# Moving the on-chip tiles of a one-core transformer-layer kernel to other places modulo 512 bytes, by pads

## The chip, the cores and the metric

The kernel runs on one core of one Trainium2 chip. The metric is the time of one execution on the device in microseconds (us); smaller is better. Each time is a median of several runs. Beside the timed runs there is one profiled execution, whose trace gives each instruction's start and shown length.

The engines are named as in the profile: PE is TensorE (matmuls and transposes), PEld its loading of weights, DVE is VectorE, ACT is ScalarE, POOL is GpSimd, SP is SyncE (which issues DMAs). All but PE's results, which go to PSUM, lies in SBUF: 128 partitions, in each of which a tile has a start address and a number of bytes.

## The reference

One layer of a hybrid decoder on x of shape (1, 1024, 1024), all in float32, with a feed-forward width of 2816:

```python
xn = rmsnorm(x, norm_mix_w[l])
proj = xn @ w_in[l]
da_q, da_k, da_v, sw_q, sw_k, sw_v, g_da, g_sw = split_cols(proj)
...
y_da = diff_attention(da_q, da_k, da_v, lam, lam_init, subln_w[l])
y_sw = sliding_window_attention(sw_q, sw_k, sw_v, sinks[l])
merged = jax.nn.sigmoid(g_da) * (y_da @ w_br_da[l]) + jax.nn.sigmoid(g_sw) * (y_sw @ w_br_sw[l])
x = x + merged @ w_mix_out[l]
xn = rmsnorm(x, norm_ffn_w[l])
x = x + conv_ffn(xn, w_up[l], conv_w[l], conv_b[l], w_down[l])
...
return rmsnorm(x, norm_final_w)
```

The matrix products with `w_in`, the two branch weights, `w_mix_out`, `w_up` and `w_down` hold nearly all of the arithmetic.

## The kernel before, in words

**A product.** Every float32 operand is split into a high and a low part of type fp32r (`xh`, `xl` of an activation, `wh`, `wl` of a weight), and a product is the sum of three matmuls: high by high, high weights by low activations, low weights by high activations. In `mm3` these are lines 150, 151 and 152, in `product` lines 835, 836 and 837. The weights are 128 x 128, the moving operand is 128 partitions by 512 columns of 4 bytes (2048 bytes a partition), and the result is one PSUM bank.

**Strassen-Winograd.** Pairs of output tiles in `project` (nine pairs), in `hidden` (22 rounds) and in the middle of `down` are computed with seven half-size products P1 to P7 in place of eight. The weight operands are `A11`, `A12`, `A22` (slices of the weights as they are) and `S1` to `S4` (sums and differences of them, tiles `sh` and `sl`, made in `split_pair`, L101). The moving operands are `B11`, `B21`, `B22` and `T1` to `T4`. The order in a round is P1, P2, P5, P6, P7, P3, P4, with 12 matmuls each; in the last pair or round another order holds.

```python
prods = (("P1", "A11", "B11"), ("P2", "A12", "B21"), ("P5", "S1", "T1"), ("P7", "S3", "T3"),
         ("P3", "S4", "B22"), ("P6", "S2", "T2"), ("P4", "A22", "T4"))
```

**The stages**, in order of time:

- `project`: x by `w_in`. Three plain tiles first (`blocks`, L276 to L278, and `mm3`), then the pairs.
- `attention`: scores (L568), transposes (L584, L677), and products with v, with the eleven remaining gate tiles of `w_in` (`back_half`, L491, which calls `mm3` with `xh`, `xl`) put between them.
- the branch products in `rest` (`yh`, `yl` by `w_br`), then `mix` (`mh`, `ml` by `w_mix_out`), both by `mm3` into tiles `sc`.
- `hidden`: the normed x by `w_up`, with `product`; the convolution and the gate of each round run on the other engines beside the next round's matmuls.
- `down`: `hd` by `w_down`: whole pieces first (L1023), then Strassen-Winograd products, then plain runs of 24 matmuls each (`mms`, L996), and the last norm.

The order of instructions is that of the program's text; the Tile layer adds the waits. TensorE has one instruction queue and takes its matmuls in this order.

**Where tiles lie.** SBUF is handed out in pools from two ends. A pool opened with `side="right"` takes addresses from the upper end down, any other one from the lower end up; each pool starts where the pool opened before it on that side ended. Pools are closed and their room is used again. The first thing that `run` does (L180 to L182) is to open one pool on each side with a single tile of `LPAD` or `RPAD` bytes a partition. No instruction reads or writes these tiles; they only move everything after them. The pools of the left, in the order of the addresses: `cp` and `st` (constants, `ident`, `vecs`, `rstd`, small tiles), `wp` (L202: raw weights, `wh`, `wl`), then those of the stages: `uwa` (in `project`: weights `sh`, `sl`), `sfa`, `xrp`, `tpa`; `gp`; `yrp`, `yp` (`yh`, `yl`), `bp`; `cpl`, `xc` (`B11`, `B21`, `B22`, `T13`), `sfp`, `xtp`; `hrp`, `hp` (parts of `hd`). Those of the right: `xp` (`xh`, `xl`), `tx` (`t13`, `t42`), `ap`, `fyp`, `mp` (`mh`, `ml`), `xc2` (`T42`), `uw` (in `hidden`: weights `sh`, `sl`), `tp`, `x3p`, `uwd` and `hpb` (in `down`).

In the trace a moving operand and the weights of a matmul are named by their tiles: `t<-B_0h,sh` has moving `B_0h` and weights `sh`. B stands for `B11`, `B21` or `B22`, T for `T13` or `T42`, in the names with numbers left out.

Of the kernel before, what the change touches and what calls it, by code (L numbers as in the profile page):

```python
# [10 lines left out]
F32 = mybir.dt.float32  # L11
# [6 lines left out]
P = 128  # L18
# [10 lines left out]
STORE = (1,9)  # L29
DEFER = (4,8)  # L30
N1 = 6
LPAD, RPAD = 480, 480
LAM_INIT = 0.2

HALVES = ((2,), (0, 0, 0, 0, 1, 1, 0, 0), (0, 0, 0, 0, 1, 0, 0, 1), (0, 0, 0, 0, 1, 0, 1, 0), (0, 0, 0, 1, 1, 0, 1, 0), (1, 0, 0, 1, 0, 1, 1, 0), (1, 0, 1, 1, 0, 0, 1, 0), (3,))
# [7 lines left out]
class Trunk:  # L43
# [132 lines left out]
    def run(self):  # L176
        nc, tc = self.nc, self.tc
        with ExitStack() as ctx:

            for side, n in (("left", LPAD), ("right", RPAD)):  # L180
                pad = ctx.enter_context(tc.tile_pool(name=f"pad_{side}", bufs=1, side=side))
                pad.tile([P, n // 4], F32, name=f"pad_{side}_t")  # L182
            self.cp = ctx.enter_context(tc.tile_pool(name="cp", bufs=1))
            self.st = ctx.enter_context(tc.tile_pool(name="st", bufs=4))
            self.dp = ctx.enter_context(tc.tile_pool(name="dp", bufs=1, space=DRAM))
            self.ident = self.cp.tile([P, P], F32, name="ident")
            make_identity(nc, self.ident)
            self.ones = self.cp.tile([P, 1], F32, name="ones")
            nc.gpsimd.memset(self.ones, 1.0)
            self.mhalf = self.cp.tile([P, 8], F32, name="mhalf")  # L190
            nc.gpsimd.memset(self.mhalf, -0.5)
            self.vecs = self.cp.tile([P, NVEC], F32, name="vecs")

            warm = self.cp.tile([P, 1], F32, name="warm")
            nc.scalar.activation(warm, self.ones, AF.Exp)
            nc.scalar.dma_start(self.vecs, self.vecs_d)
            self.rstd = self.cp.tile([P, T], F32, name="rstd")
            self.gd = self.dp.tile([16, P, T], F32, name="gd")
            self.x2d = self.dp.tile([8, P, T], F32, name="x2d")
            self.hd = self.dp.tile([NF, P, T], F32, name="hd")  # L200
            self.yd = self.dp.tile([8, P, T], F32, name="yd")
            self.wp = ctx.enter_context(tc.tile_pool(name="wp", bufs=2))  # L202
            self.qd = self.dp.tile([18, 2, P, T], F32, name="qd")
            self.xctx = ExitStack()
            self.xp = self.xctx.enter_context(tc.tile_pool(name="xp", bufs=1, side="right", reuse_waits="tile"))
            self.plan()
            self.project()
            self.pctx = ExitStack()
            self.psS = self.pctx.enter_context(tc.tile_pool(name="psS", bufs=2, space=PSUM, reuse_waits="tile"))
            self.psG = self.pctx.enter_context(tc.tile_pool(name="psG", bufs=2, space=PSUM, reuse_waits="tile"))  # L210
            self.psT = self.pctx.enter_context(tc.tile_pool(name="psT", bufs=2, space=PSUM, reuse_waits="tile"))
            gctx = ExitStack()
            self.gpool = gctx.enter_context(tc.tile_pool(name="gp", bufs=2, reuse_waits="tile"))
            self.attention()
            self.rest(gctx)
# [995 lines left out]
```

## Time and profile before

| what | value |
|---|---|
| time, median of 3 runs (lowest, highest) | 1365.05 us (1364.79, 1365.61) |
| span of the profiled execution | 1364.3 us |
| instructions in it | 17160 |
| TensorE: busy, instructions | 1345.2 us, 6304 |
| VectorE, ScalarE, GpSimd: busy | 1015.9, 603.9, 485.5 us |
| moved by DMA | 179.50 MB |

The profiled execution's span stands beside the timed runs for its own time; it is 0.75 us below their median.

How to read the profile: an engine's busy time is the sum over its instructions as the trace shows them, and a share is that of the span. The clock row gives, for each of 40 equal slices of the span, the TensorE clock that was granted, in tenths of full speed, 9 being 90% or more. The waits list which engine stood idle ahead of which instruction, and what released it. The chain of waits follows the work that ended last back from the end. In a listing in order of time, a matmul has its start, its shown length, engine, line, operands, the sizes of weights (128*128) and of the moving operand (128x512). Matmuls are pipelined, so that the next one starts before the shown end of the one ahead. A few records of matmuls can be missing from a trace.

### The profile page before, as it was taken

What the parts mean: (1) busy time and instruction counts of PE and PEld (TensorE: products, weight loads), DVE (VectorE), ACT (ScalarE), POOL (GpSimd) and SP (SyncE); (2) the same over time, 40 slices, a digit from 0 to 9 for tenths busy, and PEclk for the clock granted to TensorE, in tenths of its full rate; (3) what the DMA queues carried; (4) which work ended last, traced back from release to release, by engine and by line L of the source; (5) the groups of instructions that cost most, each with busy time, mean ns of one, the idle gap of its engine ahead of it and who ended that gap; (6) DMA issues with size and microseconds to landing.
All of it is one profiled execution on the core that took longest, in us unless ns stands there. A gap on an engine that the chain in (4) does not pass through costs nothing.

```text
span 1364.3 us, 17160 instructions
## 1 busy us (share of the span) xinstructions
PE 1345.2 (99%) x6304; PEld 1104.3 (81%) x6304; DVE 1015.9 (74%) x1454; ACT 603.9 (44%) x942; POOL 485.5 (36%) x350
## 2 busy tenths in 40 slices
PE   8999999999999999999999999999999999999997
PEld 6888888888887778878878888888888888888887
DVE  8747775388898875455689889888988888976454
ACT  8432232276667674334444333433344335332343
POOL 0336652010102135642455565556555611131011
PEclk9999999999999999999999999999999999999999
DMA  7334343966554235334522222222222238651242
GB/s 254 139 106 173 137 147 118 271 173 178 154 132 144 82 118 220 110 124 129 165 78 93 77 78 93 67 88 78 93 77 79 85 136 316 206 179 59 93 133 84
DMA packets 62469, 179.50 MB, mean 132 GB/s; under 512 B 6832, under 2 KB 15152, under 8 KB 62384
## 3 DMA queue, kind: packets, MB, share of 16 engines
q1 hardware_dynamic: 50928, 160.98, 36.5%
q10 hardware_dynamic: 11456, 17.41, 3.5%
q8 instruction: 50, 0.82, 0.2%
q14 instruction: 35, 0.29, 0.1%
HBM read 129.61 MB, written 48.76 MB: 131 GB/s over the span
## 4 chain that ended last, share of the span: by engine, by line
PE 86%; DVE 5%; POOL 3%; DMA 3%; issue 1%; ACT 1%; POOLq 0%; SPq 0%; ACTq 0%; DVEq 0%
PE t L837 14%; PE t L836 14%; PE t L835 14%; PE d L996 3%; PE y L996 3%; PE sc L568 3%; PE g L150 3%; PE g L151 3%; PE g L152 3%; DMA gr<-gd 2%; PE sc L152 2%; PE sc L150 2%; PE sc L151 2%; PE d L1023 2%; PE y L1023 2%; POOL gr L742 2%
## 5 line engine op out<-in xcount | busy, mean ns | idle before, releaser
L970 ACT ACTIVATE c<-us,vecs 128x1024 f32<-128x1024 f32 x44 | 54.7, 1246 | 162.6 <-POOL us L965 159.1
L965 POOL TENSOR_TENSOR us<-us,rstd 128x1024 f32<-128x1024 f32 x42 | 100.9, 2420 | 54.7 <-DVE wl L131 36.4
L110 ACT CAST sh<-sf 128x1024 fp32r<-128x1024 f32 x62 | 64.7, 1047 | 108.4 <-POOL sf L97 59.7
L129 ACT CAST wh<-raw 128x1024 fp32r<-128x1024 f32 (+2 forms) x60 | 60.7, 1011 | 108.6 <-PE sc L151 33.6
L131 DVE TENSOR_TENSOR wl<-raw,wh 128x1024 fp32r<-128x1024 f32 (+2 forms) x60 | 75.8, 1263 | 41.5 <-ACT wh L129 31.6
L971 DVE SCALAR_TENSOR_TENSOR c<-us,vecs,c 128x1024 f32<-128x1024 f32 x44 | 67.2, 1530 | 52.0 <-ACT c L970 52.0
L96 POOL TENSOR_TENSOR sf<-rv 128x512 f32<-128x512 f32 x30 | 43.0, 1434 | 166.6 <-DMA rv<-in_w_up 62.6
L112 DVE TENSOR_TENSOR sl<-sf,sh 128x1024 fp32r<-128x1024 f32 x62 | 90.5, 1462 | 8.6 <-ACT sh L110 8.4
L167 POOL TENSOR_TENSOR rs<-ms,mhalf 128x8 f32<-128x8 f32 (+2 forms) x9 | 14.5, 1615 | 161.2 <-DVE ms L165 150.6
L150 PE MATMUL g<-xh,wh 128*128 128x512 f32 x176 | 70.6, 401 | 0.1
L152 PE MATMUL g<-xh,wl 128*128 128x512 f32 x176 | 70.5, 401 | 0.0
L151 PE MATMUL g<-xl,wh 128*128 128x512 f32 x176 | 70.3, 399 | 0.0
L98 POOL TENSOR_TENSOR sf<-raw,rv 128x512 f32<-128x512 f32 x30 | 41.7, 1391 | 61.1 <-DVE sl L112 61.1
L572 DVE CUSTOM_DVE_ANT_0 L<-sc,bias 128x128 f32<-128x128 f32 (+7 forms) x64 | 47.7, 751 | 17.0 <-PE sc L568 13.8
L551 POOL MEMSET aT<- 128x128 f32 x32 | 6.2, 206 | 151.8 <-PE t L597 101.3
L97 POOL TENSOR_TENSOR sf<-sf,raw 128x512 f32<-128x512 f32 x31 | 58.1, 1875 | 1.7
L573 ACT ACTIVATE L<-L,sm 128x128 f32<-128x128 f32 (+7 forms) x64 | 49.6, 778 | 20.3 <-DVE sm L572 17.7
L972 DVE SCALAR_TENSOR_TENSOR c<-us,vecs,c 128x1024 f32<-128x1024 f32 x44 | 56.1, 1278 | 0.6
L725 POOL TENSOR_TENSOR gr<-gr,rstd 128x1024 f32<-128x1024 f32 x16 | 40.4, 2528 | 41.4 <-DMA gr<-gd 41.0
L112 DVE TENSOR_TENSOR wl<-raw,wh 128x1024 fp32r<-128x1024 f32 (+1 forms) x35 | 54.8, 1565 | 0.2
L150 PE MATMUL sc<-mh,wh 128*128 128x512 f32 x128 | 50.4, 394 | 0.0
L152 PE MATMUL sc<-mh,wl 128*128 128x512 f32 x128 | 50.2, 392 | 0.0
(444 smaller groups left out, 4358.8 us busy)
## 6 DMA issues: line engine op xcount, KB each, us to landing
u<-qd SPq DMA_DIRECT2D x72, 256.0 KB, 6.4
raw<-in_w_down SPq DMA_DIRECT2D x27, 512.0 KB, 3.7
raw<-in_w_in SPq DMA_DIRECT2D x25, 512.0 KB, 3.9
hr<-hd SPq DMA_DIRECT2D x50, 256.0 KB, 5.5
raw<-in_w_up SPq DMA_DIRECT2D x23, 512.0 KB, 3.5
hd<-c SPq DMA_DIRECT2D x22, 512.0 KB, 2.8
rv<-in_w_up SPq DMA_DIRECT2D x21, 512.0 KB, 3.5
gr<-gd SPq DMA_DIRECT2D x16, 512.0 KB, 3.6
```

Of the source, the lines that this page charges most:

```text
L110: nc.scalar.copy(hi, src)
L112: nc.vector.tensor_tensor(lo, src, hi.bitcast(F32), ALU.subtract)
L131: self.lo = (eng or nc.vector).tensor_tensor(wl, raw, wh.bitcast(F32), ALU.subtract)
L150: nc.tensor.matmul(ps, wh[:, kc + o, :], ah, start=first and n == 0, stop=False)
L151: nc.tensor.matmul(ps, wh[:, kc + o, :], al, start=False, stop=False)
L152: nc.tensor.matmul(ps, wl[:, kc + o, :], ah, start=False, stop=last and n == len(kcs) - 1)
L835: nc.tensor.matmul(ps, ah[:, k, :], bh, start=first and n == 0, stop=False, skip_group_check=skip)
L836: nc.tensor.matmul(ps, ah[:, k, :], bl, start=False, stop=False, skip_group_check=skip)
L837: nc.tensor.matmul(ps, al[:, k, :], bh, start=False, stop=last and n == len(ks) - 1, skip_group_check=skip)
L965: i = (nc.vector if m % NF == 0 else nc.gpsimd).tensor_tensor(us[:, 2:], us[:, 2:], self.rstd, ALU.mult)
L971: nc.vector.scalar_tensor_tensor(c, us[:, 1:T + 1], cw[1], c, ALU.mult, ALU.add)
L996: nc.tensor.matmul(ps, v[:, n, :], x, start=n == i == 0, stop=n == len(js) - 1 and i == 2)
```

## The change

The pads' sizes change, and a third pad is put on the left behind `wp`, so that the pools opened later on that side move by its size as well. No instruction, wait, queue, order or tile size is touched.

```diff
-LPAD, RPAD = 480, 480
+LPAD, MPAD, RPAD = 288, 128, 736
...
             self.wp = ctx.enter_context(tc.tile_pool(name="wp", bufs=2))
+            pad = ctx.enter_context(tc.tile_pool(name="pad_middle", bufs=1))
+            pad.tile([P, MPAD // 4], F32, name="pad_middle_t")
             self.qd = self.dp.tile([18, 2, P, T], F32, name="qd")
```

In the words of the change: pads place weights at 0, the other tiles from the left at 128 and those from the right at 256, modulo 512 bytes. "Weights" are the tiles of the pool `wp`.

## The prediction

> **What bounds the kernel now.** I read the page first, then the waits of TensorE, then its instructions in order of time. The page's first lines, its clock row and the first line of its chain say that one engine holds the end from first to last:
>
> ```profile
> span 1364.3 us, 17160 instructions
> PE 1345.2 (99%) x6304; PEld 1104.3 (81%) x6304; DVE 1015.9 (74%) x1454; ACT 603.9 (44%) x942; POOL 485.5 (36%) x350
> ...
> PEclk9999999999999999999999999999999999999999
> ...
> PE 86%; DVE 5%; POOL 3%; DMA 3%; issue 1%; ACT 1%; POOLq 0%; SPq 0%; ACTq 0%; DVEq 0%
> ```
>
> The two longest rows of TensorE's waits (who waited, for whom, us in total, times, longest):
>
> ```profile
> PE t L276 <- ACT wh L129: 6.7, 1, 6.7
> PE d L173 <- POOL rs L167: 1.0, 1, 1.0
> ```
>
> TensorE is busy 99% of the span at full clock and waits some ten microseconds. So the time is a count of matmuls times the spacing at which they follow each other, and only a change of that spacing can move the end by more than a few microseconds. The busy time of one matmul is of no use here: its shown end lies behind the next one's start. I take differences of starts. Here are starts in the hidden stage (start us, us, engine, line, operands), each at the head of a product of 12 matmuls:
>
> ```profile
> 799.90 0.39 PE L835 MATMUL t<-T_0h,sh 128*128 128x512 f32 x1
> ...
> 802.71 0.39 PE L835 MATMUL t<-B_0h,sh 128*128 128x512 f32 x1
> ...
> 805.50 0.40 PE L835 MATMUL t<-T_0h,wh 128*128 128x512 f32 x1
> ...
> 808.30 0.40 PE L835 MATMUL t<-B_0h,wh 128*128 128x512 f32 x1
> ...
> 811.06 0.39 PE L835 MATMUL t<-B_0h,wh 128*128 128x512 f32 x1
> ...
> 813.78 0.40 PE L835 MATMUL t<-T_0h,sh 128*128 128x512 f32 x1
> ...
> 816.58 0.39 PE L835 MATMUL t<-T_0h,sh 128*128 128x512 f32 x1
> ...
> 819.35 0.39 PE L835 MATMUL t<-T_0h,sh 128*128 128x512 f32 x1
> ```
>
> By the order in `hidden` these are P7, P3, P4, P1, P2, P5, P6 and the next P7. They take 2.81, 2.79, 2.80, 2.76, 2.72, 2.80 and 2.77 us: 233 ns a matmul in P7, P3, P4 and P5, 230 in P1 and P6, 226.7 in P2. Same engine, same shape, same count. What differs is where the operands lie.
>
> **Where they lie.** The edit moves everything from the left by 288 - 480 = -192 B, what comes after the middle pad by 128 B more, and everything from the right by 256 B. Since weights (`wp`) are then at 0, other left tiles at 128 and right tiles at 256, all modulo 512, they are now at 192, 192 and 0. Matmul operands are slices at multiples of 512 B, so a tile's place holds for all of them. I call offset the weights' place less the moving operand's. P1 and P2 (left by `wp`) have offset 0. P7, P3 and P5 (left by `sh` from the right) have 320. P4 (right by `wp`) has 192, P6 (right by right) 0. So: offset 0 runs at 226.7 once settled, and P1 and P6, which follow products of another offset, pay 0.04 to 0.05 us to get there; offset 320 runs at 233.3; P4 at 192 runs at 233.3 too, but elsewhere 192 does better. In the projection stage (starts of P4, P5 and the next P4) and in the mix stage:
>
> ```profile
> 142.30 0.39 PE L835 MATMUL t<-t42h,wh 128*128 128x512 f32 x1
> ...
> 150.54 0.39 PE L835 MATMUL t<-t13h,sh 128*128 128x512 f32 x1
> ...
> 161.53 0.39 PE L835 MATMUL t<-t42h,wh 128*128 128x512 f32 x1
> ```
> ```profile
> 610.33 0.39 PE L150 MATMUL sc<-mh,wh 128*128 128x512 f32 x1
> ...
> 615.82 0.39 PE L150 MATMUL sc<-mh,wh 128*128 128x512 f32 x1
> ```
>
> There 36 matmuls take 8.24 us, the next 48 take 10.99, and 24 of the mix 5.49: 228.9 ns each, all at offset 192 (`sh` of the projection comes from the left pool `uwa`). And the left by `wp` matmuls of the down stage, from the chain of waits (start us, us, what), with the rows of one shape that set the branch stage beside them:
>
> ```profile
> 1285.38 5.44 PE d L996 x24
> ```
> ```profile
> L996 PE MATMUL d<-h,wh 128*128 128x512 f32 x112 | 34.7, 391 | 0.0
> L150 PE MATMUL sc<-yh,wh 128*128 128x512 f32 x64 | 24.9, 389 | 0.0
> L150 PE MATMUL g<-xh,wh 128*128 128x512 f32 x176 | 70.6, 401 | 0.1
> ```
>
> 5.44 / 24 = 226.7 ns at offset 0, and the branch's `yh`, with the same shown length (389 against 391 ns), is taken at the same.
>
> **A rule that speaks against the change.** The Trainium skill's page "SBUF — State Buffer", section "Who interferes with whom", gives TensorE two independent read ports, one for the moving operand and one for weights, and says that it never waits for another user. By that page no place of an operand could matter and the sum below would be 0. The rows above differ by 6.6 ns, or 3%, among equal matmuls; the trace does not agree.
>
> **The change part by part.** The pads run no instruction and add no wait or DMA. They use 288 + 128 + 736 = 1152 B a partition in place of 960. Every tile keeps its pool and neighbours; every offset but one changes. Counted from the loops, in matmuls 512 wide:
>
> 1. *Left by `wp`*, 528 in `hidden` (24 a round, 22 rounds), 384 in the branch stage, 546 in `down`: offset 0 becomes 384.
> 2. *Left by right weights*, 792 in `hidden`, 108 in `down`: 320 becomes 128.
> 3. *Right by `uwa` weights*, 480 in `project`: 192 becomes 384.
> 4. *Right by `wp`*, 516 in `project`, 528 gates (the last row above), 384 in the mix, 264 in `hidden`, 222 in `down`: 192 becomes 256.
> 5. *Right by right*, 264 in `hidden`, 84 in `down` and the attention: stays 0.
>
> No row shows 128, 256 or 384. Each is bounded by the rows: 226.7 ns below, 233.3 above. 128 and 384 are both 128 B away from 0 in a ring of 256. I take them at the upper end, 233.3: the nearest shown place from 384 is 320, which is at 233.3 in every product, and 128 lies 64 B from 192, shown at 233.3 and at 228.9. For 256 I take the lower end, 226.7, as for 0. The reason is this: the two even spacings, 226.7 and 233.3, are 6.6 ns apart, and a moving operand of 2048 B goes by in about 220 ns, so that a step that came around only every 512 B would be worth 55 ns, not 6.6; a short turn is likelier than a long one, and with a short turn 256 repeats 0. This is the weakest choice; both ends stay in the range.
>
> The sum, by those choices:
> - Group 1: P1 and P2 together take 813.78 - 808.30 = 5.48 us for 24, 228.3 ns; 528 x 5.0 ns = 2.6 us. Branch and down: 930 x 6.6 = 6.1. Together **+8.7**.
> - Group 3: 480 x (233.3 - 228.9) = **+2.1**.
> - Group 2: 233.3 stays, **0**. Group 5: **0**.
> - Group 4: in `project` the runs of 36 now settle first as P1 does, 2.76 + 2 x 2.72 = 8.20 against 8.24 us, nine times, -0.4, and 192 outside the pairs at 2.2 ns, -0.4; gates 528 x 2.2, -1.2; mix 384 x 2.2, -0.8; P4 goes from 2.80 to P6's 2.77, 22 times, -0.7; down 222 x 2.2, taken from 228.9, -0.5. Together **-4.0**.
>
> Net +6.8 us. The gates and branch count in full although attention has small waits, since TensorE's row of waits is short; if those covered them, the net would be +5.5.
>
> Costed at nothing: DMA, whose start places are multiples of 64 B before and after, hidden behind a TensorE at 99%; were each of the 3% of the chain that is DMA to grow by a tenth, 4 us would show. VectorE, ScalarE and GpSimd operands move as well. They are hidden while TensorE has the next product queued; in `hidden` VectorE is the next one to matter:
>
> ```profile
> 690.00:1120.00 430.00, 429.30 (x1864) 347.55 (x1863) 374.62 (x362) 172.27 (x190) 236.32 (x171) 1.00 0.24 81
> ```
>
> Of 430 us VectorE is busy 374.62 (third number after the length), so its work could grow by an eighth before it set the pace. Transposes (128 columns, identity moving) also change their offset:
>
> ```profile
> L584 PE MATMUL t<-ident,L 128*128 128x128 f32 x144 | 22.2, 274 | 0.1
> L677 PE MATMUL t<-ident,L 128*128 128x128 f32 x120 | 19.9, 278 | 1.0 <-DVE L L670 0.3
> ```
>
> No row tells what offset does to them. The nearest two differ by 4 ns, and 264 x 4 ns is 1 us either way; I take 0.
>
> The base is the profiled execution: span 1364.3 us, 0.75 less than the median of the three runs, 1365.05 (1364.79 to 1365.61). Forecast: 1365.05 + 6.8 = **1371.9 us**.
>
> **The rivals.**
>
> *±128 B is as good as 0* (the other side). Then groups 1 and 3 go to 226.7 and group 2, the slow 900, gains 6.6 ns each. Group 1: P1 loses its settling, -0.8; group 2 -5.9; group 3 480 x 2.2, -1.1; group 4 needs no settling, -3.1 for project, gates and mix, -1.7 for P4, -0.5 down; P6 settled, -1.1. Sum -14.2: 1350.9 us. For it: places 128 B off could be a turn of their own. Against it: 320, the nearest shown to 384, is never fast. The point from which it decides: groups 1 to 3 are 2838 matmuls at a mean of 229.5 ns now; with group 4's -4.0 us the change breaks even when ±128 runs at 229.5 + 4000/2838 = 230.9 ns.
>
> *±128 B runs like 192 in the projection*, at 228.9. Group 1 +0.3 +2.0, group 2 -4.0, group 3 0, group 4 -4.0: -5.7, 1359.4 us. For it: 192 shows that a second, lower pace can hold at an offset that is not 0. Against: P4 has the same offset and stays at 233.3.
>
> *256 is not 0 but as slow as 320.* Group 4 then costs 4.4 x 1428 = +6.3 and +1.0 in `down`; with groups 1 and 3, +18.1: 1383.2 us. For it: the half turn is the farthest from 0 if the turn is 512. Against: the argument on the turn above.
>
> *Places do not matter* and the spacing belongs to the product: 1365. For it: P4 and the projection differ at one offset, so something beside place plays. Against: P5 and P6 are the same line with the same kinds of tiles, and differ.
>
> **How the numbers follow.** Forecast (1366.5 to 1377): 0.40. 256 slow (1377 to 1388): 0.18. ±128 like 192 (1355 to 1364): 0.17. ±128 like 0 (1346 to 1355): 0.17. No change: 0.08. A measurement of this kernel can tell about 0.2%, 2.7 us, from no change, so faster means under 1362.3 and slower over 1367.8. Faster: 0.17 and most of 0.17, 0.32. Same: 0.08 and the edges, 0.10. Slower: 0.58. The range 1351 to 1383 leaves out about half of the fastest case and half of the slowest, 0.18; cases of both signs are in it, and the likeliest alone has 1366.5 to 1377.
>
> **What would show it.** Starts of the same products: P2 and the L996 rows of 24 go from 2.72 and 5.44 us to 2.80 and 5.60; 24 of the mix from 5.49 to 5.44; P3 stays at 2.79; the projection's 48 go from 10.99 to 11.20 and its 36 from 8.24 to 8.20. If P3 falls towards 2.72, ±128 is good and the sign turns; if the mix rises to 5.60, 256 is not 0. Longer waits of TensorE, or a lower clock row, would mean that something other than spacing decided, and the working above would not hold.

## The result

| kernel | median (lowest to highest), runs | span of the profiled execution |
|---|---|---|
| before | 1365.51 us (1363.09 to 1366.87), 18 | 1364.3 us |
| changed | 1368.2 us (1367.47 to 1369.69), 18 | 1366.3 us |

The ratio of the changed kernel to the one before is 1.0023 (95% interval 1.0016 to 1.0030): slower by some 3.1 us, 2.2 to 4.1. The forecast was +6.8 us. The sign was right, and the size was more than twice what came.

The page of the changed kernel: span, busy times, the clock row, and the chain by engine.

```profile
span 1366.3 us, 17160 instructions
PE 1348.8 (99%) x6304; PEld 1106.1 (81%) x6304; DVE 1014.7 (74%) x1454; ACT 604.1 (44%) x942; POOL 484.1 (35%) x350
...
PEclk9999999999999999999999999999999999999998
...
PE 95%; DVE 3%; DMA 1%; issue 1%; ACT 1%; POOL 0%; POOLq 0%; ACTq 0%; SPq 0%; DVEq 0%
```

The same instructions, the same clock but for an 8 in the last of the 40 slices, and TensorE busy 99% of the span as before. So the answer lies in the spacing again. Lines 203 and below stand two lines further down than in the kernel before (L835 is now L837). The heads of the products of one hidden round, in order of time (start us, length us, engine, line, operands):

```profile
799.94 0.40 PE L837 MATMUL t<-T_0h,sh 128*128 128x512 f32 x1
...
802.74 0.40 PE L837 MATMUL t<-B_0h,sh 128*128 128x512 f32 x1
...
805.53 0.39 PE L837 MATMUL t<-T_0h,wh 128*128 128x512 f32 x1
...
808.27 0.40 PE L837 MATMUL t<-B_0h,wh 128*128 128x512 f32 x1
...
811.06 0.40 PE L837 MATMUL t<-B_0h,wh 128*128 128x512 f32 x1
...
813.86 0.40 PE L837 MATMUL t<-T_0h,sh 128*128 128x512 f32 x1
...
816.66 0.39 PE L837 MATMUL t<-T_0h,sh 128*128 128x512 f32 x1
...
819.40 0.40 PE L837 MATMUL t<-T_0h,sh 128*128 128x512 f32 x1
```

P7, P3, P4, P1, P2, P5 and P6 take 2.80, 2.79, 2.74, 2.79, 2.80, 2.80 and 2.74 us. P1 and P2, now 128 B off, went from 2.76 and 2.72 to the slow pace; P4, now 256 B off, from 2.80 to 2.74, and P6 with it, from 2.77. P7, P3 and P5, moved from 320 to 128 B, stayed. A round takes 19.46 us, before 19.45: in the hidden stage loss and gain cancel.

The projection (P4, P5, the next P4), the branch stage (24 matmuls), the mix (24), and the chain's piece of 24 in the down stage:

```profile
141.95 0.39 PE L837 MATMUL t<-t42h,wh 128*128 128x512 f32 x1
...
150.12 0.40 PE L837 MATMUL t<-t13h,sh 128*128 128x512 f32 x1
...
161.27 0.39 PE L837 MATMUL t<-t42h,wh 128*128 128x512 f32 x1
```
```profile
543.77 0.40 PE L150 MATMUL sc<-yh,wh 128*128 128x512 f32 x1
...
549.34 0.39 PE L150 MATMUL g<-yh,wh 128*128 128x512 f32 x1
```
```profile
605.68 0.39 PE L150 MATMUL sc<-mh,wh 128*128 128x512 f32 x1
...
611.12 0.39 PE L150 MATMUL sc<-mh,wh 128*128 128x512 f32 x1
```
```profile
1286.42 5.60 PE d L998 x24
```

The projection's 36 went from 8.24 to 8.17 us and its 48 from 10.99 to 11.15; 24 of the mix from 5.49 to 5.44; 24 of the down stage from 5.44 to 5.60; 24 of the branch stage now take 5.57, 232.1 ns each. Each of these groups moved the way that was forecast.

### The profile page after: what moved, and what is told of

The parts are those of the page before. It is cut to its first block, busy times and chain, and to the rows that moved or that the text cites. A ratio compares the mean times of both kernels' runs of the same rounds, so it can differ in the third digit from the quotient of the medians.

```text
span 1366.3 us, 17160 instructions
## 1 busy us (share of the span) xinstructions
PE 1348.8 (99%) x6304; PEld 1106.1 (81%) x6304; DVE 1014.7 (74%) x1454; ACT 604.1 (44%) x942; POOL 484.1 (35%) x350
## 4 chain that ended last, share of the span: by engine, by line
PE 95%; DVE 3%; DMA 1%; issue 1%; ACT 1%; POOL 0%; POOLq 0%; ACTq 0%; SPq 0%; DVEq 0%
PE t L838 14%; PE t L839 14%; PE t L837 14%; PE g L150 4%; PE g L151 4%; PE g L152 4%; PE d L998 3%; PE y L998 3%; PE sc L151 3%; PE sc L152 3%; PE sc L150 3%; PE sc L570 3%; PE d L1025 2%; PE y L1025 2%; PE t L586 1%; PE d L837 1%
## 5 line engine op out<-in xcount | busy, mean ns | idle before, releaser
L151 PE MATMUL sc<-ml,wh 128*128 128x512 f32 x128 | 49.9, 390 | 0.0
```

The costliest lines, as they stand in the source:

```text
L151: nc.tensor.matmul(ps, wh[:, kc + o, :], al, start=False, stop=False)
```

## The experiments

Theory: the spacing of 512-column matmuls hangs on the weights' place less the moving operand's, modulo 256 B. Rivals: the place of one operand alone; a period of 512 B; the traffic of the other engines.

**The disputed cost by itself (m1_places).** The kernel leaves out the whole layer and runs this block, 48 matmuls with n and KC both 4, at 48 pairs of places (w and x are slices of one weights tile and one moving tile):

```python
                for r in range(n):
                    for k in range(KC):
                        nc.tensor.matmul(ps, w(k, 0), x(k, 0), start=r == k == 0, stop=False)
                        nc.tensor.matmul(ps, w(k, 0), x(k, 1), start=False, stop=False)
                        nc.tensor.matmul(ps, w(k, 1), x(k, 0), start=False, stop=r == n - 1 and k == KC - 1)
```

> This kernel leaves out the whole layer: it runs only 48 blocks of 48 matmuls of 512 columns, in the order high by high, high by low, low by high, from one weights tile and one moving tile, with the other engines idle. Blocks 1 to 16 move the weights' place by 0, 32, 64, 96, 128, 160, 192, 224, 256, 320, 384, 448, 4, 16, 48 and 112 B, blocks 17 to 32 the moving operand's, blocks 33 to 48 both. Theory 'difference modulo 256' (spacing hangs on the weights' place less the moving operand's, modulo 256 B): 226.7 ns at 0 and 256, 232.4 to 233.1 at 128 and 384, all sixteen of the third set at 226.7, and the second set the mirror of the first (p there like 512 - p here), 64 and 192 at 233.3 and 228.9. Rival 'one operand's place alone': one of the first two sets is flat and the third is not. Rival 'the other engines' traffic': all 48 blocks alike, since nothing else runs.

The heads of blocks 3 to 13, in which the weights move and the moving operand stays, in order of time. The offsets are 64, 96, 128, 160, 192, 224, 256, 320, 384, 448 and 4 B:

```profile
36.88 0.40 PE L35 MATMUL b<-X,W 128*128 128x512 f32 x1
...
48.08 0.39 PE L35 MATMUL b<-X,W 128*128 128x512 f32 x1
...
59.32 0.39 PE L35 MATMUL b<-X,W 128*128 128x512 f32 x1
...
70.48 0.40 PE L35 MATMUL b<-X,W 128*128 128x512 f32 x1
...
81.68 0.40 PE L35 MATMUL b<-X,W 128*128 128x512 f32 x1
...
92.67 0.40 PE L35 MATMUL b<-X,W 128*128 128x512 f32 x1
...
103.87 0.39 PE L35 MATMUL b<-X,W 128*128 128x512 f32 x1
...
114.75 0.40 PE L35 MATMUL b<-X,W 128*128 128x512 f32 x1
...
125.94 0.39 PE L35 MATMUL b<-X,W 128*128 128x512 f32 x1
...
137.10 0.40 PE L35 MATMUL b<-X,W 128*128 128x512 f32 x1
...
148.10 0.39 PE L35 MATMUL b<-X,W 128*128 128x512 f32 x1
```

The differences over 48 give 233.3 ns at 64, 234.2 at 96, 232.5 at 128, 233.3 at 160, 229.0 at 192, 233.3 at 224, 226.7 at 256, 233 at 320, 232.5 at 384 and 229.2 at 448. The row repeats after 256 B: 64 as 320, 128 as 384, 192 as 448, and 256 at the pace of 0. With the moving operand moved in place of the weights the row comes out mirrored (229 ns where the moving operand is 64 B ahead, 233.3 where it is 64 B behind). With both moved together by multiples of 32 B, all twelve blocks settle at 226.7. The other four, 4, 16, 48 and 112 B off, did not, against the expectation (the last section has the first two). So for places at multiples of 32 B, as the kernel's are, it is the difference that counts, and the rivals of one operand and of other engines' traffic fall: beside these matmuls VectorE was busy for 1.4 us of the whole run. The Trainium skill's page "SBUF — State Buffer", section "Who interferes with whom", gives TensorE two independent read ports and says that it never waits for another user; it does not cover this: here TensorE is alone, and equal matmuls range from 226.7 to 234.2 ns.

**256 B against 0 (e2_right_0, e3_left_0), and all at 0 (e1_all_0).**

```diff
-LPAD, MPAD, RPAD = 288, 128, 736   # changed kernel
+LPAD, MPAD, RPAD = 288, 128, 480   # e2_right_0
+LPAD, MPAD, RPAD = 288, 0, 736     # e3_left_0, no middle pad
+LPAD, MPAD, RPAD = 288, 0, 480     # e1_all_0, no middle pad
```

> The changed kernel with right tiles at 0 in place of 256, so that offsets are 384, 128 and 0 as before but 256 nowhere. Theory 'difference modulo 256': nothing changes, each group keeps its spacing within 0.3 ns, ratio to the kernel before 1.002 (1368 us). Rival 'modulo 512': 0 and 256 differ, groups 3 and 4 move by over 1 ns a matmul, over 2 us.

1367.93 us, ratio 1.0029 (1.0019 to 1.0039). From the starts, the mean spacing of each group of over 100 matmuls, waits left out, lies within 0.2 ns of the changed kernel's, but for 0.5 ns in the 144 matmuls of the down stage's products with weights from `wp`. The period of 512 B falls.

> The changed kernel without the middle pad: weights 0, left 0, right 256. Theory 'difference modulo 256': all offsets are 0 or 256, the time is that of all at 0 (1351 to 1354 us) within 0.1%, and the whole loss of the change against this version, some 15 us, belongs to the 128 B. Rival 'modulo 512': group 2 (offset 256) and group 4 (256) stay off 226.7 and it is over 3 us above the version with all at 0.

> Weights, other left tiles and right tiles all at 0. Theory 'difference modulo 256': every block of products settles at 226.7 ns; the 900 of group 2 gain 6.6 ns each (-5.9 us), groups 3, 4 and 5 gain 2.2 to 6 ns each, together -14 us by the rival's sum in the prediction, less about 2 us that waits of the branch and mix stages take back: 1351 to 1354 us. Rival 'one operand's place alone': groups 2 and 4 exchange nothing with each other, so at most one of them gains: above 1358 us.

1354.13 us, ratio 0.9930 (0.9917 to 0.9942), and 1354.51 us, ratio 0.9929 (0.9916 to 0.9941), beside a kernel before of 1363.88. The two agree, as the period of 256 B wants. They gained 9.6 us, where the rival's sum in the prediction has 14.2 and the expectation some 12. Group 2 did settle at 226.7 ns (mean 226.8, from 233.3) and gained 5.2 us in the hidden stage. Most of what went missing stands at the head of the hidden rounds; the last of the experiments follow it.

**The whole layout moved by 64 B (e4_shift_64).**

```diff
-LPAD, MPAD, RPAD = 288, 128, 736
+LPAD, MPAD, RPAD = 224, 128, 800
```

> The changed kernel with everything moved by 64 B: weights 448, left 64, right 192, so that all differences stay as in the changed kernel. Theory 'difference modulo 256': every group keeps its spacing within 0.3 ns and the ratio to the kernel before stays at 1.002 to 1.003. Rival 'absolute places': groups move by over 1 ns and the time by over 2 us either way.

1368.14 us, ratio 1.0033 (1.0021 to 1.0046). The same groups' spacings are those of the changed kernel within 0.4 ns, most within 0.1. Absolute places do not count.

**Other differences (e5_left_64, e7_right_448).**

```diff
-LPAD, MPAD, RPAD = 288, 128, 736   # changed kernel
+LPAD, MPAD, RPAD = 288, 64, 480    # e5_left_64
-LPAD, RPAD = 480, 480              # kernel before
+LPAD, RPAD = 480, 544              # e7_right_448
```

> Weights 0, left 64, right 0. The differences are 192 modulo 256 in groups 1 and 2, 64 in group 3, 0 in groups 4 and 5. Theory 'difference modulo 256', with the spacings of the kernel of places (192: 228.9, 64: 233.3, 0: 226.7): group 1 +2.0, group 2 -4.0, group 3 +2.1, group 4 -3.7, group 5 -0.4, in sum -4.0 us, ratio 0.997. Rival 'any place off 0 is as slow as 233': group 1 as in the changed kernel (+7.5), group 2 as before, +5 us, ratio 1.004.

1362.09 us, ratio 0.9987 (0.9978 to 0.9996): 1.8 us faster, half of the forecast. Group 2 went to 229.4 ns and group 3 to 233.3, as expected; group 1 went to 229.1 in the down stage and 229.6 in the hidden stage, but to 233.0 in the branch stage. One offset thus has two paces. The rival of a single slow pace falls too.

> The kernel before with its right pad alone raised by 64 B: weights 192, left 192, right 448, so that every difference is 0 or 256. Theory 'difference modulo 256': the same as with all tiles at 0, ratio 0.993 within 0.001, all groups but the gates at 226.7 to 227.7 ns. Rival 'absolute places or modulo 512': over 3 us away from it.

1356.16 us, ratio 0.9941 (0.9928 to 0.9953), with one number of the kernel before changed. It agrees with the versions at 0 and 256 within the intervals, 0.1% above them.

**What an offset does after another one, and to shorter matmuls (m2_follow).** This kernel too leaves out the whole layer.

> This kernel leaves out the whole layer: runs of 24 matmuls at one offset follow runs of 24 at another, all 16 pairs of 0, 64, 128 and 192, each pair twice, then 48 matmuls each of 256 and of 128 columns at the four offsets. Theory 'the pace at an offset hangs on the phase in which it is entered': 0 settles at 226.7 from each other offset after an extra 0.04 us or so, 128 lies between 232.3 and 233.4, 192 is at 228.9 when entered from 0 and can be at 233.3 when entered from another. Rival 'the offset alone sets it': each offset has one pace whatever came before it. For 256 and 128 columns no row says anything; if only the start of a matmul is concerned they show the same 6 ns at 64 and 128 as 512 columns do.

Four heads of 24 matmuls each; the blocks from 175.41 and from 186.60 us have offset 192 and follow one of 64, the one from 181.01 has 64:

```profile
175.41 0.40 PE L35 MATMUL b<-X,W 128*128 128x512 f32 x1
...
181.01 0.39 PE L35 MATMUL b<-X,W 128*128 128x512 f32 x1
...
186.60 0.40 PE L35 MATMUL b<-X,W 128*128 128x512 f32 x1
...
192.11 0.39 PE L35 MATMUL b<-X,W 128*128 128x512 f32 x1
```

Offset 192 takes 5.60 us the first time (233.3 ns) and 5.51 the second (229.6, with 228.9 once settled). After 0 or 192 it settled at 228.9 each time; of the four blocks of 192 behind one of 64, two ran at 233 and two at 229.6. Offset 128 settled between 231.6 and 233.3, offset 0 at 226.6 to 227.2 after every other one. So P4, which follows P3 at 320 (64 modulo 256), and the projection could differ at one offset in the trace of before. The prediction left this open with "something beside place plays": what ran ahead is part of it, but two and two behind the same block show that this alone does not settle it, and the rest stays open.

With 256 columns, the heads of the blocks of 48 with offsets 0, 64 and 128:

```profile
369.39 0.28 PE L35 MATMUL b<-X,W 128*128 128x256 f32 x1
...
375.15 0.28 PE L35 MATMUL b<-X,W 128*128 128x256 f32 x1
...
380.61 0.28 PE L35 MATMUL b<-X,W 128*128 128x256 f32 x1
```

Offset 0 takes 5.76 us or 120.0 ns a matmul, 64 takes 5.46 or 113.8; 128 and 192 took 118.5 and 117.7. Here 0 is the slowest and 64 the fastest. With 128 columns all four settle at 111.7 ns. What is best for 512 columns is not best for every width.

**A second profile of the kernel before (n1_before_again).**

> The kernel before once more, for a second profile of it. Theory 'spacing': the 512-column spacings are the same within 0.1 ns in every group; only waits differ. If the waits that the changed kernel's trace lacks (0.7 us at the last gate product of the branch stage, 0.6 us in the down stage, 0.9 us at the start) are there again, a slower TensorE covers them; if they are gone here too, they were chance in the first profile and its base lies high. Ratio 1.000 within 0.001.

Ratio 1.0002 (0.9993 to 1.0011), span 1362.7 us, 1.6 less than the first profile. Its spacings agree with the first profile's within 0.3 ns in all groups of over 100 but the projection's first three plain tiles, 233.6 ns in place of 229.5. Of the waits in question only one is there again:

```profile
PE y L837 <- DVE wl L131: 0.5, 1, 0.5
```

The changed kernel's waits of TensorE have no such row, nor have those of the version with the right at 0. This fits a TensorE that comes later to this product and finds VectorE done; no run shows it by itself. The wait at the gate product of the branch stage and those of the mix are gone in the second profile of before as well: they were chance, and the first profile's span lay high by them.

**The branch stage alone (e6_y_128).**

```diff
+                bctx.enter_context(tc.tile_pool(name="pad_y", bufs=1)).tile([P, 32], F32, name="pad_y_t")
                 yp = bctx.enter_context(tc.tile_pool(name="yp", bufs=1, reuse_waits="tile"))
```

> The kernel before with only the branch stage's yh and yl (and that stage's gate tiles) moved by 128 B, so that 384 matmuls have 128 in place of 0 and all else is as before. Theory 'spacing counts in full': 384 x 5.4 ns = +2.1 us in the stage and in the time, ratio 1.0015. Rival 'the branch stage's waits cover it': the spacing of these 384 rises to 232.4 all the same, but the stage grows by under 1 us, ratio under 1.0007.

1365.89 us, ratio 1.0017 (1.0008 to 1.0025), 1.1 to 3.4 us. The 384 matmuls went from 227.0 to 232.5 ns, +2.1 us. The spacing counts in full here; the rival needed under 1.0007.

**Where the gain of offset 0 stops (e8_a22_pool, e9_low_last).** In the version with all at 0, the head of P1 in three hidden rounds, the second four rounds after the first and the third fifteen after the second:

```profile
723.92 0.39 PE L837 MATMUL t<-B_0h,wh 128*128 128x512 f32 x1
...
800.08 0.39 PE L837 MATMUL t<-B_0h,wh 128*128 128x512 f32 x1
...
1089.64 0.39 PE L837 MATMUL t<-B_0h,wh 128*128 128x512 f32 x1
```

The first four take 76.16 / 4 = 19.04 us, which is 84 x 226.7 ns; the fifteen after them 289.56 / 15 = 19.30, 4.0 us more in all. One of the fifteen, by engine (start us, length, and in brackets how long the engine stood idle ahead of it and for whom):

```profile
823.86 1.29 POOL L98 TENSOR_TENSOR sf<-raw,rv 128x512 f32<-128x512 f32 x1 [2.90 <-DVE sl L112]
```
```profile
826.58 4.87 POOL L967 TENSOR_TENSOR us<-us,rstd 128x1024 f32<-128x1024 f32 x2
```
```profile
829.52 1.25 ACT L972 ACTIVATE c<-us,vecs 128x1024 f32<-128x1024 f32 x1 [7.47 <-POOL us L967]
```
```profile
830.80 1.73 DVE L973 SCALAR_TENSOR_TENSOR c<-us,vecs,c 128x1024 f32<-128x1024 f32 x1 [2.57 <-ACT c L972]
```
```profile
837.36 1.76 DVE L112 TENSOR_TENSOR wl<-raw,wh 128x1024 fp32r<-128x1024 f32 x1
```
```profile
839.17 0.19 PEld L839 LDWEIGHTS t<-B_0h,wl 128*128 128x128 f32 x1 [0.34 <-DVE wl L112]
```

GpSimd scales the round's results, ScalarE starts the convolution, VectorE goes on with it, and behind that in VectorE's queue stands the low part of the next A11 and A12, on which P1's third matmul waits. Further on in the same queue stands the low part of S1 and S2 (`sl`); GpSimd waits for it (the first line) before it makes the next differences and scales the next results, and with that the circle closes. It takes 19.3 us a round. In the version with all at 0 the low part of A11 and A12 was ready 2.98, 0.64, 0.29 and from there on 0.05 us ahead of P1's third matmul, round by round. In the kernel before it came every 19.39 us on average, against 19.44 for TensorE's round, and was ready 1.5 us ahead or more in every round. So the circle had some 0.05 us a round to spare there. Two tests start from the version with all at 0. The first takes 0.68 us off VectorE by giving the low part of A22 to GpSimd in most rounds; the second needs A11's low part later.

```diff
-        self.uw = None
+        self.uw, self.early = None, False
...
-            nc.vector.tensor_tensor(lo, src, hi.bitcast(F32), ALU.subtract)
+            (nc.gpsimd if self.early and names == ("A22",) else nc.vector).tensor_tensor(lo, src, hi.bitcast(F32), ALU.subtract)
...
+                self.early = 0 < j < NF - 3
```

> All tiles at 0, and in the rounds of the hidden stage the low part of A22 is made by GpSimd in place of VectorE (0.68 us less a round on VectorE ahead of the low part of A11 and A12, on which the first product of the next round waits). Theory 'VectorE takes 3.4 us back in the hidden stage': the waits of 0.1 to 0.25 us at the third matmul of P1 go, the group of P1 and P2 falls by some 3 us, ratio 0.990 to 0.991. Rival 'GpSimd slows VectorE beside it as much': the waits stay, ratio 0.993 or more.

1364.18 us, ratio 1.0006 (0.9997 to 1.0015): all of the gain gone, with rounds of some 19.85 us. TensorE's loads of weights in the version with all at 0, with A22 on GpSimd, and with low weights last (who waited, for whom, us in total, times, longest):

```profile
PEld t L839 <- DVE wl L112: 5.8, 15, 0.5
```
```profile
PEld t L839 <- DVE wl L112: 15.1, 17, 1.0
```
```profile
PEld t L843 <- DVE wl L112: 4.6, 11, 0.5
```

The wait of which the theory said that it would go nearly trebled. Two lines, of VectorE and of GpSimd's subtraction beside it, show the price:

```profile
834.97 2.19 DVE L975 SCALAR_TENSOR_TENSOR c<-us,vecs,c 128x1024 f32<-128x1024 f32 x1
```
```profile
833.81 2.26 POOL L112 TENSOR_TENSOR wl<-rv,wh 128x512 fp32r<-128x512 f32 x1
```

The subtraction took 2.26 us there in place of 0.68, and the step of the convolution beside it 2.19 us where its neighbours take 1.27 to 1.28: VectorE lost more by it than the 0.68 us that it was spared.

```diff
+        last_low = b == "B11" and first and last and not skip and len(ks) == 4
...
-            nc.tensor.matmul(ps, al[:, k, :], bh, start=False, stop=last and n == len(ks) - 1, skip_group_check=skip)
+            if not last_low:
+                nc.tensor.matmul(ps, al[:, k, :], bh, start=False, stop=last and n == len(ks) - 1, skip_group_check=skip)
+        for n, k in enumerate(ks if last_low else ()):
+            nc.tensor.matmul(ps, al[:, k, :], self.B[b, k][0], start=False, stop=n == len(ks) - 1, skip_group_check=skip)
```

> All tiles at 0, and in the whole P1 products of project and hidden the four matmuls with low weights come after the eight with high weights, in place of third of each three; nothing else changes. Theory 'VectorE's low part of A11 is late at the head of each round and takes about 3 us back': that low part is then needed 0.23 x 8 = 1.8 us after P1's start in place of 0.45, so the 0.1 to 0.25 us a round are hidden; the group of P1 and P2 falls by about 3 us against all tiles at 0 without this, ratio 0.990 to 0.991. Rival 'the rounds are bound by VectorE all the same': the wait moves elsewhere in the round and the ratio stays at 0.993.

1353.97 us, ratio 0.9929 (0.9916 to 0.9943), as without it. The head of P1 in three rounds, the second eight rounds after the first and the third eleven after the second:

```profile
724.82 0.39 PE L838 MATMUL t<-B_0h,wh 128*128 128x512 f32 x1
...
877.14 0.39 PE L838 MATMUL t<-B_0h,wh 128*128 128x512 f32 x1
...
1089.82 0.39 PE L838 MATMUL t<-B_0h,wh 128*128 128x512 f32 x1
```

Now eight rounds run at 152.32 / 8 = 19.04 us, and the last eleven at 212.68 / 11 = 19.33. The rival was right: a later need buys a few rounds of slack, and then the pace is that of the circle. The theory that a late low part alone was at fault fell; the circle of GpSimd, ScalarE and VectorE sets the hidden stage once TensorE needs under 19.3 us a round.

## Why the prediction was right in sign and wrong in size

The time was read as a count of matmuls times a spacing, and that held: no wait grew by more than the 0.3 us of the first, the clock stayed, and the kernel of places shows the spacing without anything else. The reading of the offsets, with 256 as good as 0 and 128 nearly as bad as 320, held also. For 256 that was in part luck: the prediction called it its weakest choice, and its reason, a step that would be worth 55 ns, is shown by no run. The runs show that the row repeats after 256 B, not what makes it. The terms of the sum, with the mean spacing of the three profiles that share these differences (the changed kernel, the one with the right at 0, the one moved by 64 B) less that of the two profiles of before:

| term | forecast, us | measured, us |
|---|---|---|
| group 1, hidden | +2.6 | +2.4 (228.3 to 233.0 ns) |
| group 1, branch and down | +6.1 | +5.2 (227.0 to 232.4; 227.4 to 233.1) |
| group 2 | 0 | -0.3 (233.3 to 233.1) |
| group 3 | +2.1 | +1.6 (to 232.5) |
| group 4, project | -0.8 | -1.3 |
| group 4, gates | -1.2 | +0.1 |
| group 4, mix, P4, down | -2.0 | -2.7 (P4 -1.4 of it) |
| group 5 | 0 | -0.5 (P6) |
| wait in the down stage | not in the sum | -0.6 |
| sum | +6.8 | +3.9 |

+3.9 us is 1.0029, inside the interval of the changed kernel and in the middle of the three kernels that share its differences (1.0023, 1.0029, 1.0033).

The step that failed is "I take them at the upper end, 233.3": the value of 128 and 384. P2, P3, P5 and the run of 24 shown from the down stage did go at 233.3, but P1 and P7 at 232.7 and the projection and the branch at 232.4: an uneven pace, with a mean of 232.4 to 233.1 ns by group, and this took 0.9 from group 1's branch and down, 0.2 from its hidden part, 0.3 from group 2 and 0.5 from group 3, 1.9 of the 2.9 us that the sum was too high. The upper end was the pace of another offset, at the edge of the bounds, and taken for 2838 matmuls at once: each tenth of a nanosecond there is 0.3 us of the sum.

Two terms of group 4 were wrong as well, in opposite directions. "P4 goes from 2.80 to P6's 2.77" took P6's time with its settling after a slow product for granted; P4 and P6 both came to 2.74. And "gates 528 x 2.2, -1.2" took 528 matmuls to be in settled runs. In the attention stage some 430 of them stand in some 120 runs, 3.5 matmuls long on average, between scores and transposes, as these lines of the changed kernel in order of time show:

```profile
332.26 0.40 PE L152 MATMUL g<-xh,wl 128*128 128x512 f32 x1
332.49 0.53 PE L570 MATMUL sc<-u,u 128*128 128x384 f32 x2
332.85 0.40 PE L150 MATMUL g<-xh,wh 128*128 128x512 f32 x1
```

Their spacing inside these runs was 230 ns before and after, and also with all at 0. In runs of three or four the better offset was worth nothing here. P6, taken at nothing, gained 0.5: behind a P5 at 128 it takes 2.74 us.

Of the waits, that the branch would "count in full" held (+2.1 us of spacing, ratio 1.0017 by itself), while in the down stage 0.6 us of the later TensorE fell into a wait for VectorE that was there anyway.

The rivals: places do matter; 256 is not slow; 128 is neither as good as 0 nor as 192 in the projection. But the price of the rival on the other side, -14.2 us, was wrong too, and so was "its work could grow by an eighth before it set the pace": VectorE's busy share of 87% hid that it waits 2.57 us a round in the middle of a circle with some 0.05 us to spare. What offset 0 everywhere is worth here is 9.6 us. Of the 4.6 that it lacks, the rows above put 4.0 down to that circle; the gates' 1.2, which did not come there either, would more than cover the rest, but no run splits it.

## What to carry to other kernels

Where TensorE is busy throughout, compare the starts of equal matmuls: a few per cent between them can come from where their operands lie. Here 512-column fp32r matmuls with weights and moving operand at the same place modulo 256 B ran at 226.7 ns and the others at 229 to 234, so one pad that brings all pools to one place is the better version (ratio 0.993), and splitting the pools by 128 B the worse one; but 256 columns had another order and 128 columns none. Before a faster pace is summed up, count only runs long enough to settle, and look for the circle of other engines that becomes the bound: its length can be read from the round, not from a busy share.

## What the runs showed of the hardware that was not expected

- The spacing of 512-column fp32r matmuls repeats with 256 B of the difference between the weights' place and the moving operand's, for places at multiples of 32 B. At one difference (192) it has two lasting paces, 228.9 and 233.3 ns; in the kernel without the layer the slow one came only behind a run at 64, and there in two of four cases.
- A moving operand off a multiple of 32 B has a price of its own even at equal places: 237.5 ns a matmul at 4 B off, 230.8 at 16 B off. At 16 B off and an offset of 400 B it was back at 226.7.
- GpSimd's subtraction of 128 x 512 elements took 2.26 us beside VectorE, which does it in 0.68 us, and the VectorE step beside it 2.19 in place of 1.28 us.
- What reads collide where in the memory was not tried; only the places were.
